# Routing traced in portions of 2.8 instead of 1.4, and gathered expert rows shared out anew between two halves of a PEER stage

## The chip, the cores and the metric

The kernel runs on one core of one Trainium2 chip. The metric is the device time of one execution in microseconds. All the times of the kernel before come from three timed runs and from one further execution that was profiled.

## The reference, cut to what matters

One decoder layer for 512 tokens of width 2048 in float32: a normalised input projection, two groups of attention heads, an output projection, and then a retrieval of experts (PEER) that is added to the result. Only the last matters here:

```python
def peer(h, w_q, sub_keys, expert_u, expert_v):
    q = (xt @ w_q).reshape(T, PEER_HEADS, 2, PEER_DQ // 2)
    s = jnp.einsum('thpd,hpnd->thpn', q, sub_keys)
    s_half, i_half = lax.top_k(s, PEER_TOPK)
    cand = s_half[:, :, 0, :, None] + s_half[:, :, 1, None, :]
    ...
    top_s, pos = lax.top_k(cand, PEER_TOPK)
    idx = jnp.take_along_axis(cand_idx, pos, axis=-1)
    g = jax.nn.softmax(top_s, axis=-1)
    ...
        u = expert_u[ic]
        a = jnp.einsum('cd,ced->ce', xc, u)
        w = (gc * jax.nn.gelu(a)).astype(xc.dtype)
        return jnp.einsum('ce,ced->cd', w, expert_v[ic])
```

Each token picks 8 x 16 = 128 of 16,384 experts. An expert has a row of `peer_u` and a row of `peer_v`, each of 2048 floats.

## The kernel before, in words

The four blocks of 128 tokens are treated in two ways. For block 0 (tokens 0 to 127) the chosen rows are fetched one slot at a time: an indirect DMA on the POOL queue (L965) brings 128 rows, one for each token, 1 MB in all, into one of three buffers `gt`. Slots 0 to 127 fetch rows of `peer_u`; VectorE forms a product with the tokens and its sum (L973, a multiply-and-reduce followed by a short read of the accumulator). Then comes one GELU (L978), and slots 128 to 255 fetch rows of `peer_v`, which VectorE adds to the result `h` (L976). These 256 steps are the generator `gathered()`. Step i asks first for the rows of step i + 2, whose buffer comes free when step i - 1 is done with it.

For blocks 1 to 3 (384 tokens, `TD`) every expert is computed densely, in two stages:

- The **U stage** is 128 blocks `u_block(e)`. One block loads 128 experts of `peer_u` (1 MB, on the SP and ACT queues, L858, two blocks ahead), VectorE transposes them in two halves (L870), ScalarE and VectorE split each half into a high and a low part (L117 and L118 in `split`), and TensorE multiplies them with the tokens: 16 steps of three matmuls with 384 columns (L883 to L885). A GELU (L890) follows, and its result goes to a scratch tensor in memory (L891, POOL queue). The halves are made three halves ahead of their matmuls (`u_turn(n + 3)`).
- The **V stage** is 16 groups of 8 such blocks. Each group multiplies `peer_v` (1024 rows, in four column pieces of 512) with weights `wg`, which are read back from the scratch tensor (L1015), multiplied by the gates on POOL (L1040), and split on ScalarE and VectorE. A group has 288 matmuls with 512 columns (L191 to L193), and VectorE adds each finished piece to the result (L1059, 12 in a group).

The gates for the dense part are made meanwhile by the generator `dense_gates()`: one-hot rows on POOL (L907), VectorE (L909) and ScalarE (L912), and two matmuls with 128 columns for each of 384 tokens (L922).

The generators are traced in pieces between other code. A `Filler` keeps a credit: `run(budget)` adds the budget, up to 4.0, and takes pieces from its queue until the credit is used up. A gathered step costs 2.3.

```python
            yield 2.3
    gatherer = Filler(paced=True)
    while filler.queue or later:
        flush(4)
        u_block(e, 1.4)
    share = 36.0 / (NK - 4 - e)
        u_block(e, share, 0.85)
                gatherer.run(1.6)
```

`u_block(e, budget, pace)` runs `filler` with `budget` and `gatherer` with `pace`, once in each of its two halves. The first loop runs until the routing (top-16 selections, `route`, L750 to L791) is traced; only then are `gathered()` and `dense_gates()` put into their queues. In the V stage the gatherer runs 16 times in a group. What is left after the last group is done by `gatherer.drain()`. A scheduler that knows the tiles decides the order of each engine's instructions from the order of the trace; a paced step is, besides, kept behind the last split or result addition (`mark`) that was traced before it.

Of the kernel before, what the change touches and what calls it, by code (L numbers as in the profile page):

```python
# [52 lines left out]
def block_kernel(ctx, tc, x, positions, norm1_gain, w_in, q_a_gain, w_q_b, kv_a_gain, w_kv_b, mla_q_gain,  # L53
# [13 lines left out]
    def pool(name, bufs=1, side=None, stack=ctx, **kw):  # L67
        return stack.enter_context(tc.tile_pool(name=name, bufs=bufs, side=side, reuse_waits="tile", **kw))
# [7 lines left out]
    def acc_tile(name="acc"):  # L76
        return psum.tile([128, 512], F32, name=name, tag="acc", bufs=5)

    def tp_tile(name="tp"):
        return psum.tile([128, 512], F32, name=name, tag="tp", bufs=3)  # L80
# [71 lines left out]
    def flush(n=None):  # L152
        for _ in range(len(later) if n is None else min(n, len(later))):
            later.pop(0)()
# [14 lines left out]
    def weights(src, kc, c0, n, by_row=False, turn=0):  # L169


        rows_of = src.rearrange("(i k j) n -> i j k n", i=4, j=32) if by_row else src.rearrange("(k p) n -> p k n", p=128)
        for k0 in range(0, kc, 4):
            kn = min(4, kc - k0)
            raw = raw_tile(turn * kc // 4 + k0 // 4)
            with tc.high_priority(offset=1500):
                if by_row:
                    for i in (0, 2, 1, 3):
                        nc.sync.dma_start(raw[32 * i:32 * i + 32, :kn, :n], rows_of[i, :, k0:k0 + kn, c0:c0 + n])
                else:  # L180
                    nc.sync.dma_start(raw[:, :kn, :n], rows_of[:, k0:k0 + kn, c0:c0 + n])
            for k in range(0, kn, 2):
                hi, lo = part_pair(turn * kc // 2 + (k0 + k) // 2, [128, 2, 512])
                with tc.high_priority(offset=1500):
                    split(hi[:, :, :n], lo[:, :, :n], raw[:, k:k + 2, :n])
                yield hi, lo

    def products(o, lhs, t, k0, kc, w, n):
        for k in range(2):
            kk = k0 + k  # L190
            nc.tensor.matmul(o, lhs(0, kk, t), w[0][:, k, :n], start=kk == 0, stop=False)  # L191
            nc.tensor.matmul(o, lhs(0, kk, t), w[1][:, k, :n], start=False, stop=False)  # L192
            nc.tensor.matmul(o, lhs(1, kk, t), w[0][:, k, :n], start=False, stop=kk == kc - 1)  # L193
# [668 lines left out]
    def u_turn(n):  # L862
        if n >= 2 * NK:
            return
        e, hf = divmod(n, 2)
        if hf == 0:
            u_load(e + 2)
        hi, lo = part_pair(n, [128, 8, 128])
        uT = up.tile([128, 8, 128], F32, name="uT")
        nc.vector.transpose(uT.rearrange("p k (b j) -> p b k j", j=32),  # L870
                            u_raw[e].rearrange("p b (k i) -> p b k i", k=KC)[:, :, hf * 8:hf * 8 + 8, :])
        split(hi, lo, uT)
        u_parts[n] = hi, lo

    def u_block(e, budget, pace=0.0):
        pa = acc_tile("pa")
        for hf in range(2):
            n = 2 * e + hf
            u_turn(n + 3)
            hi, lo = u_parts.pop(n)  # L880
            for k in range(8):
                kk = hf * 8 + k
                nc.tensor.matmul(pa[:, :TD], hi[:, k, :], xTd[0][:, kk, :], start=kk == 0, stop=False)  # L883
                nc.tensor.matmul(pa[:, :TD], hi[:, k, :], xTd[1][:, kk, :], start=False, stop=False)  # L884
                nc.tensor.matmul(pa[:, :TD], lo[:, k, :], xTd[0][:, kk, :], start=False, stop=kk == KC - 1)  # L885
            filler.run(budget)
            gatherer.run(pace)
        ga = xtp.tile([128, TD], F32, name="ga", bufs=2)
        with tc.issue_after(first[0].ins):
            nc.scalar.activation(ga, pa[:, :TD], AF.Gelu_apprx_tanh)  # L890
        nc.gpsimd.dma_start(acts_d[e], ga)  # L891
# [91 lines left out]
    gatherer = Filler(paced=True)  # L983
# [5 lines left out]
    e = 0  # L989
    while filler.queue or later:  # L990
        flush(4)
        u_block(e, 1.4)
        e += 1
    filler.add(settle())
    filler.add(first_tokens())
# [7 lines left out]
    share = 36.0 / (NK - 4 - e)  # L1003
    gts, wgs, wb = {}, {}, {}

    def gate_tile(g):
        if g < NSG:
            gg = wp.tile([128, TD, SG], F32, name="gg", bufs=2)
            nc.sync.dma_start(gg, gates_d[g].rearrange("j (t e) -> j t e", e=SG))
            gts[g] = gg  # L1010

    def act_tile(e):
        if e < NK:
            wgs[e] = wp.tile([128, TD], F32, name="wg", bufs=AHEAD)
            nc.sync.dma_start(wgs[e], acts_d[e])  # L1015
# [1 line left out]
    AHEAD = 5  # L1017
    wp = None
    while e < NK:
        u_block(e, share, 0.85)  # L1020
        e += 1
        if not filler.queue and wp is None:
            stg.close()
            wp = pool("wp", side="right")
            gate_tile(0)
            for i in range(AHEAD):
                act_tile(i)
# [5 lines left out]
    def w_block(e):  # L1033
        if e >= NK:
            return
        g, i = divmod(e, SG)
        if i == 0:
            gate_tile(g + 1)
        wg = wgs.pop(e)
        nc.gpsimd.tensor_tensor(wg, wg, gts[g][:, :, i], op=ALU.mult)  # L1040
        wb[e] = [dp.tile([128, TD], F32R, name=x, bufs=SG + 5) for x in ("wh", "wl")]
        split(wb[e][0], wb[e][1], wg)
        act_tile(e + AHEAD)
# [6 lines left out]
    for g in range(NSG):  # L1050
        for c in range(4):
            acc = [acc_tile(), acc_tile(), tp_tile()]
            for i, w in enumerate(weights(v_rows[g * SG * 128:(g + 1) * SG * 128], SG, c * 512, 512, turn=4 * g + c)):
                k0 = 2 * i
                for t in range(NT - 1):
                    products(acc[t], lambda hl, kk, t: wb[g * SG + kk][hl][:, t * 128:(t + 1) * 128], t, k0, SG, w, 512)
                    if k0 == SG - 2:
                        hc = h[t + 1][:, c * 512:(c + 1) * 512]
                        mark[0] = nc.vector.tensor_tensor(hc, acc[t], hc, op=ALU.add)  # L1059
                        if g == NSG - 1:  # L1060
                            nc.sync.dma_start(out[(t + 1) * 128:(t + 2) * 128, c * 512:(c + 1) * 512], hc)
                nxt = (g + 1) * SG
                if c < 3 and k0 < 4:
                    w_block(nxt + 2 * c + k0 // 2)
                if c == 3 and k0 > 2:
                    w_block(nxt + 4 + k0 // 2)
                gatherer.run(1.6)
    gatherer.drain()


# [23 lines left out]
```

## Time and profile before

| | |
|---|---|
| median of 3 runs | 3233.54 us (3232.82 to 3234.42) |
| the profiled execution's own time | 3233.09 us |
| its span in the profile | 3231.4 us |
| TensorE matmuls busy | 3104.4 us, 96% of the span |
| VectorE (DVE) busy | 2367.1 us, 73% |
| ScalarE (ACT) busy | 1271.4 us, 39% |
| GpSimd (POOL) busy | 1248.2 us, 39% |
| moved by DMA | 731.74 MB, 226 GB/s over the span |

The span counts from the first to the last instruction and transfer of the program. A matmul counts as busy until its modelled end, and matmuls overlap, so a busy TensorE can still have small gaps between two starts. How many matmuls a stretch holds tells more than its busy time. In the profile the U stage ends at about 2089 us, and the V stage follows.

### The profile page before, as it was taken

How to read it: one execution, taken by the hardware profiler on the slowest of the kernel's cores; microseconds unless marked ns; L12 is line 12 of the kernel's file. 1: busy time of each engine (PE TensorE's matmuls, PEld its weight loads, DVE VectorE, ACT ScalarE, POOL GpSimd, SP SyncE). 2: the span in 40 equal slices, each digit the busy share in tenths (PEclk: the TensorE clock that was granted, in tenths of full speed). 3: DMA queues.
4: the chain of work that ended last, by engine and by line, in shares of the span. 5: the costliest groups of instructions: out<-in, count | busy, mean ns of one | idle time of the engine just before them, and what ended most of it. 6: DMA issues, size and time to landing. Idle time of an engine off the chain costs nothing.

```text
span 3231.4 us, 43988 instructions
## 1 busy us (share of the span) xinstructions
PE 3104.4 (96%) x15802; PEld 2716.9 (84%) x15802; DVE 2367.1 (73%) x3502; ACT 1271.4 (39%) x2342; POOL 1248.2 (39%) x1260
## 2 busy tenths in 40 slices
PE   8999999989988999999999999999998999999997
PEld 6977768868788999999999999977776778887785
DVE  6436663247998567778778777788877989989896
ACT  5434452232234335566656554332222233222321
POOL 1115330001223015556566654254434445544542
PEclk9999999999999999999999999999999999999998
DMA  5422223243336668898879889998887999989896
GB/s 169 120 88 72 63 92 105 91 134 75 75 95 189 153 152 246 255 246 249 261 217 268 253 242 274 313 343 311 321 315 296 344 336 340 347 331 366 328 330 253
DMA packets 307068, 731.74 MB, mean 226 GB/s; under 512 B 24098, under 2 KB 106274, under 8 KB 269730
## 3 DMA queue, kind: packets, MB, share of 16 engines
q1 hardware_dynamic: 175394, 343.01, 33.8%
q0 software_dynamic: 45056, 293.63, 24.8%
q10 hardware_dynamic: 86400, 92.29, 10.9%
q8 instruction: 125, 2.05, 0.3%
q14 instruction: 93, 0.76, 0.1%
HBM read 666.97 MB, written 61.87 MB: 226 GB/s over the span
## 4 chain that ended last, share of the span: by engine, by line
PE 51%; DVE 13%; DMA 7%; issue 5%; POOL 2%; ACT 1%; ACTq 0%; SPq 0%; DVEq 0%; POOLq 0%
PE pa L883 10%; PE pa L885 10%; PE pa L884 10%; PE acc L192 4%; PE acc L193 4%; PE acc L191 4%; DMA wg<-acts_d 3%; DVE wlo L118 2%; PE gps L922 2%; DVE h L976 2%; PE tp L191 2%; PE tp L192 2%; PE tp L193 2%; DMA gt<-in_peer_u_dram,eidx 1%; DVE ulo L118 1%
## 5 line engine op out<-in xcount | busy, mean ns | idle before, releaser
L885 PE MATMUL pa<-xTd,wlo 128*128 128x384 f32 x1536 | 517.8, 339 | 12.5 <-DVE wlo L118 12.4
L883 PE MATMUL pa<-xTd,whi 128*128 128x384 f32 x1536 | 523.9, 341 | 0.2 <-ACT whi L117 0.2
L884 PE MATMUL pa<-xTd,whi 128*128 128x384 f32 x1536 | 519.1, 338 | 0.0
L118 DVE TENSOR_TENSOR wlo<-wraw,whi 128x1024 fp32r<-128x1024 f32 (+3 forms) x229 | 287.8, 1263 | 268.7 <-ACT whi L117 262.2
L907 POOL TENSOR_SCALAR oj<-iot,slT 128x128 fp32r<-128x128 f32 x384 | 351.4, 924 | 311.8 <-PE gps L922 310.4
L117 ACT ACTIVATE whi<-wraw 128x1024 fp32r<-128x1024 f32 (+3 forms) x229 | 232.6, 1022 | 503.6 <-PE acc L193 251.2
L973 DVE CUSTOM_DVE_ANT_0 gt<-gt,xn 128x2048 f32<-128x2048 f32 x128 | 297.6, 2325 | 53.9 <-DMA gt<-in_peer_u_dram,eidx 53.8
L976 DVE SCALAR_TENSOR_TENSOR h<-gt,w,h 128x2048 f32<-128x2048 f32 x128 | 319.7, 2497 | 18.3 <-DMA gt<-in_peer_v_dram,eidx 18.1
L118 DVE TENSOR_TENSOR wlo<-uT,whi 128x1024 fp32r<-128x1024 f32 x192 | 238.1, 1246 | 125.6 <-ACT whi L117 123.5
L192 PE MATMUL acc<-wlo,wh 128*128 128x512 f32 x768 | 306.7, 399 | 15.4 <-DVE wlo L118 15.3
L965 POOL DMA_INDIRECT gt<-in_peer_v_dram,eidx x128 | 220.2, 1720 | 256.7 <-DVE h L976 223.6
L1040 POOL TENSOR_TENSOR wg<-wg,gg 128x384 f32<-128x384 f32 x128 | 228.8, 1800 | 225.5 <-DMA wg<-acts_d 213.3
L191 PE MATMUL acc<-whi,wh 128*128 128x512 f32 x768 | 305.6, 398 | 5.0 <-ACT wh L117 5.0
L193 PE MATMUL acc<-whi,wl 128*128 128x512 f32 x768 | 305.4, 398 | 0.4 <-DVE wl L118 0.4
L885 PEld LDWEIGHTS pa<-xTd,wlo 128*128 128x128 f32 x1536 | 290.7, 189 | 13.9 <-DVE wlo L118 13.9
L883 PEld LDWEIGHTS pa<-xTd,whi 128*128 128x128 f32 x1536 | 291.3, 190 | 0.4 <-ACT whi L117 0.3
L884 PEld LDWEIGHTS pa<-xTd,whi 128*128 128x128 f32 x1536 | 291.0, 189 | 0.0
L912 ACT ACTIVATE oi<-on,gT 128x128 fp32r<-128x128 bf16 x768 | 250.6, 390 | 95.7 <-issue 24.4
L117 ACT ACTIVATE whi<-uT 128x1024 fp32r<-128x1024 f32 x192 | 200.8, 1053 | 141.0 <-PE pa L884 35.6
L965 POOL DMA_INDIRECT gt<-in_peer_u_dram,eidx x128 | 176.0, 1375 | 180.8 <-DVE a L973 158.8
L191 PE MATMUL acc<-whi,xT 128*128 128x512 f32 (+2 forms) x624 | 238.9, 383 | 4.7 <-ACT xT L117 2.3
L192 PE MATMUL acc<-wlo,xT 128*128 128x512 f32 (+2 forms) x624 | 233.5, 374 | 8.5 <-DVE wlo L118 8.4
(300 smaller groups left out, 6790.1 us busy)
## 6 DMA issues: line engine op xcount, KB each, us to landing
wraw<-in_peer_v_dram SPq DMA_DIRECT2D x86, 1024.0 KB
wraw<-in_peer_u_dram ACTq DMA_DIRECT2D x172, 256.0 KB
wraw<-in_peer_u_dram SPq DMA_DIRECT2D x172, 256.0 KB
uraw<-in_peer_v_dram SPq DMA_DIRECT2D x42, 1024.0 KB
acts_d<-ga POOLq DMA_DIRECT2D x128, 192.0 KB
gates_d<-stage ACTq DMA_DIRECT2D x24, 1024.0 KB
gg<-gates_d SPq DMA_DIRECT2D x16, 1536.0 KB
wg<-acts_d SPq DMA_DIRECT2D x128, 192.0 KB
```

Of the source, the lines that this page charges most:

```text
L117: first[0] = nc.scalar.activation(hi, src, AF.Copy)
L118: mark[0] = nc.vector.tensor_tensor(lo, src, hi.bitcast(F32), op=ALU.subtract)
L191: nc.tensor.matmul(o, lhs(0, kk, t), w[0][:, k, :n], start=kk == 0, stop=False)
L192: nc.tensor.matmul(o, lhs(0, kk, t), w[1][:, k, :n], start=False, stop=False)
L193: nc.tensor.matmul(o, lhs(1, kk, t), w[0][:, k, :n], start=False, stop=kk == kc - 1)
L883: nc.tensor.matmul(pa[:, :TD], hi[:, k, :], xTd[0][:, kk, :], start=kk == 0, stop=False)
L884: nc.tensor.matmul(pa[:, :TD], hi[:, k, :], xTd[1][:, kk, :], start=False, stop=False)
L885: nc.tensor.matmul(pa[:, :TD], lo[:, k, :], xTd[0][:, kk, :], start=False, stop=kk == KC - 1)
L907: nc.gpsimd.tensor_scalar(oj, iot, slT[1][:, t:t + 1], None, op0=ALU.is_equal)
L965: nc.gpsimd.indirect_dma_start(out=gt, out_offset=None, in_=u_rows if i < SLOTS else v_rows, in_offset=bass.IndirectOffsetOnAxis(ap=eidx0[ ...
L973: nc.vector.tensor_tensor_reduce(out=gt, in0=gt, in1=xn0, scale=1.0, scalar=0.0, op0=ALU.mult, op1=ALU.add, accum_out=a[:, s:s + 1])
L976: nc.vector.scalar_tensor_tensor(h[0], gt, w[:, s:s + 1], h[0], op0=ALU.mult, op1=ALU.add)
```

## The change

Three numbers change. The first loop of U blocks gives routing 2.8 for each half block instead of 1.4, so that it takes about half as many blocks. The second loop gives the gatherer 1.2 for each half block instead of 0.85. The V stage gives it 1.3 instead of 1.6 in each of its 16 turns in a group. `share`, the dense gates' part of each half block, is computed from the block that the second loop begins with, and so becomes smaller by itself.

```diff
@@ -989,7 +989,7 @@
     e = 0
     while filler.queue or later:
         flush(4)
-        u_block(e, 1.4)
+        u_block(e, 2.8)
         e += 1
     filler.add(settle())
     filler.add(first_tokens())
@@ -1017,7 +1017,7 @@
     AHEAD = 5
     wp = None
     while e < NK:
-        u_block(e, share, 0.85)
+        u_block(e, share, 1.2)
         e += 1
         if not filler.queue and wp is None:
             stg.close()
@@ -1064,7 +1064,7 @@
                     w_block(nxt + 2 * c + k0 // 2)
                 if c == 3 and k0 > 2:
                     w_block(nxt + 4 + k0 // 2)
-                gatherer.run(1.6)
+                gatherer.run(1.3)
     gatherer.drain()
```

The order of instructions shows it at three places of VectorE's queue. In it `uT` is a transposed half of a U block, `whi`/`wlo` and `uhi`/`ulo` are its parts, `on` a one-hot row of the dense gates, and `xn` the tokens of block 0. The first place is the U stage at blocks 22 to 24, before the change:

```order
 L870 STREAM_TRANSPOSE uT<-wraw 128x4x8x32 x2
 L118 TENSOR_TENSOR ulo<-uT,uhi 128x1024
 L118 TENSOR_TENSOR wlo<-uT,whi 128x1024
 L870 STREAM_TRANSPOSE uT<-wraw 128x4x8x32
 L870 STREAM_TRANSPOSE uT<-uraw 128x4x8x32
 L118 TENSOR_TENSOR wlo<-uT,whi 128x1024 x2
```

and with it:

```order
 L870 STREAM_TRANSPOSE uT<-wraw 128x4x8x32 x2
 L909 TENSOR_SCALAR on<-iotb,slT_9235 128x128 x4
 L118 TENSOR_TENSOR ulo<-uT,uhi 128x1024
 L118 TENSOR_TENSOR wlo<-uT,whi 128x1024
 L973 ISA gt,a<-gt,xn_5857 128x2048
 L973 ISA a 128x1
 L870 STREAM_TRANSPOSE uT<-wraw 128x4x8x32
 L870 STREAM_TRANSPOSE uT<-uraw 128x4x8x32
```

Gates and gathered rows now stand there from block 16 on instead of block 32. Counted up to the last transpose of the U stage, VectorE has 72 steps L973 before and 116 with the change. Up to the tenth block, where the routing ends, its queue reads the same in both. The second place is the third group of the V stage, before:

```order
 L973 ISA gt,a<-gt,xn_5857 128x2048
 L973 ISA a 128x1
 L118 TENSOR_TENSOR ulo<-uraw,uhi 128x1024
 L118 TENSOR_TENSOR wl<-wg,wh 128x384
 L973 ISA gt,a<-gt,xn_5857 128x2048
 L973 ISA a 128x1
 L118 TENSOR_TENSOR wlo<-wraw,whi 128x1024
 L118 TENSOR_TENSOR wl<-wg,wh 128x384 x2
 L973 ISA gt,a<-gt,xn_5857 128x2048
```

and with the change:

```order
 L118 TENSOR_TENSOR wl<-wg,wh 128x384 x3
 L118 TENSOR_TENSOR wlo<-wraw,whi 128x1024 x3
 L1059 TENSOR_TENSOR hd_21146<-acc,hd_21146 128x512
 L1059 TENSOR_TENSOR hd_21148<-acc,hd_21148 128x512
 L1059 TENSOR_TENSOR hd_21150<-tp,hd_21150 128x512
 L976 SCALAR_TENSOR_TENSOR h_4852<-gt,w,h_4852 128x2048
 L118 TENSOR_TENSOR ulo<-wraw,uhi 128x1024
 L976 SCALAR_TENSOR_TENSOR h_4852<-gt,w,h_4852 128x2048
```

Before, the rows of `peer_u` (L973) reach into the fifth group, 13 in the first and 9 to 12 in the others. With the change the last 12 of them stand in the first group, together with the GELU and the first row of `peer_v` (L976); then these rows follow at 9 in a group, where before there are mostly 11. The third place is the end of the program, before:

```order
 L1059 TENSOR_TENSOR hd_21014<-acc,hd_21014 128x512
 L1059 TENSOR_TENSOR hd_21016<-acc,hd_21016 128x512
 L1059 TENSOR_TENSOR hd_21018<-tp,hd_21018 128x512
 L976 SCALAR_TENSOR_TENSOR h_4852<-gt,w,h_4852 128x2048 x5
 L1090 UNCONDITIONAL_BRANCH
```

and with the change:

```order
 L118 TENSOR_TENSOR ulo<-wraw,uhi 128x1024
 L1059 TENSOR_TENSOR hd_21146<-acc,hd_21146 128x512
 L1059 TENSOR_TENSOR hd_21148<-acc,hd_21148 128x512
 L1059 TENSOR_TENSOR hd_21150<-tp,hd_21150 128x512
 L1090 UNCONDITIONAL_BRANCH
```

The five gathered steps that stood behind the last result addition are gone from there; the last gathered step now stands early in the last group.

## Rows read from the trace of the kernel before

**Rows 1.** Windows: stretch, busy time and instructions of each engine, clock, DMA share, GB/s.

```profile
1068.00:1200.00 132.00, 132.00 (x766) 132.00 (x765) 74.39 (x67) 42.70 (x56) 11.00 (x20) 1.00 0.64 149
1425.00:2022.00 597.00, 596.45 (x3629) 596.07 (x3628) 448.95 (x612) 351.27 (x800) 349.68 (x381) 1.00 0.86 251
2022.00:2089.00 67.00, 65.95 (x381) 65.63 (x379) 55.52 (x48) 21.50 (x27) 22.77 (x21) 1.00 0.96 307
2089.00:2173.00 84.00, 78.88 (x327) 62.09 (x328) 63.29 (x64) 26.30 (x37) 40.49 (x28) 0.98 0.90 340
2173.00:2479.00 306.00, 283.01 (x1172) 223.05 (x1171) 245.06 (x237) 84.60 (x101) 124.84 (x79) 0.98 0.83 310
2479.00:2881.00 402.00, 400.35 (x1714) 321.03 (x1713) 359.85 (x279) 121.49 (x143) 203.46 (x111) 1.00 0.91 338
2881.00:3211.00 330.00, 327.70 (x1400) 262.04 (x1398) 287.42 (x226) 91.31 (x103) 145.70 (x85) 1.00 0.89 331
```

**Rows 2.** Windows of the gates' matmuls L922 alone: PE and weight loads.

```profile
1425.00:2022.00 597.00, 77.18 (x552) 81.40 (x552) 1.00 0.86 251
```

**Rows 3.** Windows of L973 alone (two instructions a step): VectorE.

```profile
1425.00:2022.00 597.00, 107.93 (x94) 1.00 0.86 251
2022.00:2089.00 67.00, 18.34 (x16) 1.00 0.96 307
2173.00:2479.00 306.00, 101.88 (x86) 0.98 0.83 310
```

**Rows 4.** Windows of L976 alone: VectorE.

```profile
2479.00:2881.00 402.00, 165.09 (x65) 1.00 0.91 338
```

**Rows 5.** Groups by line on VectorE, 1425 to 2022 us: busy, mean ns, idle before.

```profile
L118 DVE TENSOR_TENSOR wlo<-uT,whi 128x1024 fp32r<-128x1024 f32 x95 | 116.9, 1230 | 67.6 <-ACT whi L117 65.9 <-ACT ga L890 1.6
L973 DVE CUSTOM_DVE_ANT_0 gt<-gt,xn 128x2048 f32<-128x2048 f32 x47 | 107.5, 2288 | 0.0
L973 DVE DVE_READ_ACCUMULATOR2_ANT a<- 128x1 f32 x47 | 3.8, 81 | 0.0
```

**Rows 6.** Waits, 2173 to 2479 us: total, times, longest, in us.

```profile
DVE gt L973 <- DMA gt<-in_peer_u_dram,eidx: 46.4, 12, 7.5
...
PE acc L192 <- DVE wlo L118: 12.7, 7, 4.8
PE acc L192 <- DVE ulo L118: 10.2, 6, 4.9
```

**Rows 7.** Waits, 2479 to 2881 us.

```profile
DVE h L976 <- DMA gt<-in_peer_v_dram,eidx: 6.4, 5, 2.6
...
PE acc L192 <- DVE ulo L118: 1.6, 2, 1.2
```

**Rows 8.** Timeline, third V group: start, duration, engine, instruction, idle before.

```profile
2260.00 2.29 DVE L973 CUSTOM_DVE_ANT_0 gt<-gt,xn 128x2048 f32<-128x2048 f32 x1 [4.89 <-DMA gt<-in_peer_u_dram,eidx]
...
2258.30 0.40 PE L191 MATMUL acc<-whi,wh 128*128 128x512 f32 x1
2263.49 0.62 PE L192 MATMUL acc<-wlo,wh 128*128 128x512 f32 x1 [4.80 <-DVE wlo L118]
2263.91 0.63 PE L193 MATMUL acc<-whi,wl 128*128 128x512 f32 x1
```

**Rows 9.** Timeline, end of the program: VectorE, then the SP queue.

```profile
3210.61 0.69 DVE L1059 TENSOR_TENSOR hd<-tp,hd 128x512 f32<-128x512 f32 x1 [0.71 <-PE tp L193]
3211.22 7.12 DVE L976 SCALAR_TENSOR_TENSOR h<-gt,w,h 128x2048 f32<-128x2048 f32 x3
...
3224.09 2.35 DVE L976 SCALAR_TENSOR_TENSOR h<-gt,w,h 128x2048 f32<-128x2048 f32 x1 [0.26 <-DMA gt<-in_peer_v_dram,eidx]
...
3194.53 17.13 SPq L1061 DMA_DIRECT2D out_dram<-hd  x4
3226.47 0.33 SPq L981 DMA_DIRECT2D out_dram<-h  x1
```

**Rows 10.** One line's instructions, L973: shortest, median and longest ns.

```profile
L973 DVE CUSTOM_DVE_ANT_0 gt<-gt,xn x128: 2272/2284/3957, 1007.9 to 2459.5; 128x2048 f32<-128x2048 f32 x128
```

## The prediction

> **What bounds the kernel now.** I read the windows first, because the change moves work between two stages. In the U stage TensorE is the bound. The stretch from 1068 to 1200 us has neither gates nor more than one gathered row: 766 matmuls in 132 us, 0.1723 us each [rows 1]. From 1425 to 2022 us gates and rows are added. Of its 3629 matmuls 552 are the gates' [rows 1, 2]. The other 3077 at 0.1723 us make 530.2 us, and the remaining 66.8 us are less than the 77.2 us for which the gate matmuls count as busy. So there is no room for stalls. VectorE is busy for 449 of these 597 us, 75% [rows 1]; its 47 gathered steps found their data there each time (no idle time before them), while it waited 65.9 us for ScalarE's high parts [rows 5]. A wait there costs nothing as long as the parts are ready ahead of TensorE.
>
> In the V stage the same count shows where time is lost. From 2479 us to 3211 us there are 1714 + 1400 = 3114 matmuls in 732 us, 0.2351 us each. From 2173 to 2479 us there are 1172, which would be 275.5 us at that pace, and it took 306: **30.5 us lost**. The first group, 2089 to 2173 us, has 327 matmuls, 76.9 us at that pace: 7.1 us lost [rows 1]. The waits name the cause in the slow stretch. VectorE waited 46.4 us in 12 waits for gathered rows of `peer_u`, and TensorE waited for VectorE's low parts, 12.7 and 10.2 us [rows 6]. One case can be followed in the timeline: a step L973 sat 4.89 us until its rows landed, the split behind it in the queue came late, and TensorE stood from 2258.3 to 2263.5 us. After it matmuls start 0.42 us apart [rows 8], nearly twice the usual spacing, which is the lower of the clock's two levels (1.2 instead of 2.4 GHz); the granted clock of the stretch is 0.98. In the next stretch, 2479 to 2881 us, rows are even denser, 65 steps in 402 us [rows 4] against 43 in 306 [rows 3], yet VectorE waited 6.4 us for them and TensorE 1.6 us for VectorE [rows 7].
>
> At the end the last result addition is over at 3211.3 us. Five gathered steps follow, the last begins at 3224.09 us, the write of `h` is issued at 3226.47 us, and the span ends at 3231.4 us [rows 9]. That is a **tail of 20.1 us** after the last work of the dense part.
>
> **The change, part by part.** No instruction is added or removed; the 256 gathered steps, the routing and the gates stay as many as they were.
>
> *Routing in larger portions.* VectorE's queue is the same up to the end of the routing, so nothing is gained there directly. Its effect is that gates and rows start some 16 blocks earlier, in a stretch where VectorE is busy 56% and the DMA engines 64% of the time [rows 1]. The gates' matmuls cost TensorE the same wherever they stand: 0.
>
> *44 more steps in the U stage.* The order has 116 instead of 72 up to the last transpose. One costs VectorE 2.288 + 0.081 = 2.37 us [rows 5], together 104 us. They are spread over about 112 blocks, some 1020 us. Before there were 47 steps in 597 us, now 116 in 1020; that is 0.035 more per us and 8% more of VectorE, so 83%. There is a stretch that shows this load already: from 2022 to 2089 us there are 8 steps in 67 us [rows 3], VectorE is busy 55.5 us, 83%, and 381 matmuls at 0.1723 us fill 65.6 of the 67 us [rows 1]. The bounds are 0 and 104 us (each added step paid in full). That nearest row loses 1.4 us in 67, part of which is the change of stage; scaled to 1020 us it gives 21 us as a cautious value. I take **+4 us**, near the lower end, because 1425 to 2022 us shows no loss at all.
>
> *Their transfers.* A step brings 1.05 MB, so 0.035 more per us adds 37 GB/s to 251. The 288 GB/s are below the 307 that the stretch from 2022 to 2089 us carries without a stall, and below the 338 of the V stage [rows 1]. 0. On POOL each added gather stands between the gates' one-hot rows; POOL is busy 350 of 597 us [rows 1], and in the idle 41% of 1020 us each of 44 added steps could take 9 us. 0. If that cover fails, it shows as gate matmuls that come late, and TensorE has other matmuls between them.
>
> *Groups 2 to 5 of the V stage.* All rows of `peer_u` but 12 are gone from the stage; at 9 rows of `peer_v` in a group it has fewer than the later groups have now. I price these groups at the pace of the later ones, and leave a little for waits like those of [rows 7] (6.4 us in 402, so some 4 in 306): 30.5 - 4 = **26.5 us gained**. The bounds are 0 and 30.5.
>
> *The first group.* It keeps 12 of 13 steps L973, and takes in the GELU, which waits for the last of them and stands on ScalarE ahead of later splits. Gates that end some blocks earlier may help. Between a gain of the 7.1 us lost there now and one more wait as long as the longest, 7.5 us [rows 6]; I take 0.
>
> *The later groups.* 9 steps instead of 11 give VectorE more air, but TensorE sets the pace there already: 0.
>
> *The tail.* The last addition is followed by the write of a quarter of a megabyte instead of five steps and the write of 1 MB. That write took 4.9 us; I take 4 us for the smaller one, between 0 and 4.9. 20.1 - 4 = **16 us gained**.
>
> The sum is 4 - 26.5 + 0 - 16 = -38.5 us on the profiled execution's 3233.1 us, **3195 us** rounded. That execution lies 0.45 us under the median of the runs. The forecast's own range is 3180 (no loss in U, the first group smooth, nothing lost in groups 2 to 5: 4 + 7.1 + 4 us less) to 3212 us (21 us lost in U instead of 4).
>
> **The rivals.** *First: the slow groups are slow because they begin the V stage, not because of the rows of `peer_u`.* For it speaks that denser rows do no harm later [rows 4, 7], so something else must differ, as the first weights `wg` that have to come back from memory. Against it: the waits name `peer_u` transfers, and it is a long start that lasts four groups. Then only the tail is gained: 3233.1 - 16 + 4 = 3221 us.
>
> *Second, and slower: in the U stage VectorE is already the pace-maker behind the scenes.* Its idle quarter is then no room but a loop with ScalarE (a transpose, the high part, the low part), with 65.9 us of waits in 597 [rows 5], and an added step lengthens the block. Paid in full that is 104 us against the 42.5 gained: 3233.1 - 42.5 + 104 = 3295 us. It decides once more than 42.5 of 104, 41%, are exposed. Against it speak the matmul counts above, above all 2022 to 2089 us.
>
> *Third: VectorE and POOL hinder each other.* A step L973 takes 2284 ns in the median and 3957 at most [rows 10], so something can stretch it by 1.67 us. If all 116 in the U stage were stretched like that, VectorE would have 194 us more in 1020, 19% on top of 83%, and the stage would be 2% over, some 26 us: 3233.1 - 42.5 + 26 = 3217 us. Against it: the mean in the U stage is 2288 ns [rows 5] with POOL busy more than half the time. The Trainium skill, "SBUF — State Buffer", section "SBUF: two separate sides", states a rule of this kind: an instruction of VectorE with two SBUF inputs and a GpSimd instruction that reads SBUF take an exclusive lock on one shared port pair, and the loser waits for the whole instruction. By that rule more such steps beside the one-hot rows of POOL would be longer; the mean of this trace does not bear it out for these.
>
> **How the numbers follow.** Forecast 0.70, first rival 0.13, second 0.09, third 0.03. The remaining 0.05 is for gains and losses that cancel to within 0.2% (6.5 us), about what a measurement of this kernel can tell from no change. So faster 0.70 + 0.13 + 0.03 = 0.86, the same 0.05, slower 0.09. The range reaches from 3176 to 3225 us: it takes in the forecast's own range, the third rival and the first, and leaves out the slower one and the cancelling cases.
>
> **What would show it.** Right: L973 between the U blocks from about block 16, with a mean under 2.4 us; the U stage's matmuls without gates still at 0.172 to 0.174 us; the last addition L1059 as the last work of VectorE, followed by one write; from the second V group on about 0.235 us for each matmul, and no long waits for gathered rows. Wrong: TensorE waiting for low parts in the U stage (second rival); groups 2 to 5 still losing 30 us without L973 in them (first rival); L973 well over 2.4 us there (third).

## The result, and the profile of the changed kernel

The changed kernel takes 3204.56 us in the median of four runs (3198.46 to 3209.73), the kernel before 3233.18 us on the same chip (3230.99 to 3234.42). The ratio is 0.9912 with a 95% interval of 0.989 to 0.9933: **0.9% faster**. The forecast was 3195 us, so it is 9.6 us too low. The profiled execution took 3209.73 us with a span of 3207.7 us, 23.7 us less than before. It is the slowest of the four; where the others were faster, up to 11.3 us, no profile shows.

The windows of the changed kernel, with the same columns as [rows 1]; the stages are cut where its U stage (2114 us) and its V groups end:

```profile
1200.00:2035.00 835.00, 818.49 (x4891) 814.80 (x4890) 669.41 (x850) 442.41 (x977) 436.90 (x497) 0.99 0.92 279
2035.00:2114.00 79.00, 78.88 (x456) 78.56 (x454) 66.94 (x59) 24.28 (x30) 22.09 (x20) 1.00 0.97 287
2114.00:2208.00 94.00, 83.62 (x341) 64.48 (x342) 74.30 (x71) 29.64 (x42) 48.59 (x30) 0.98 0.88 334
2208.00:2469.00 261.00, 261.00 (x1120) 210.07 (x1119) 227.32 (x179) 81.04 (x95) 116.06 (x69) 1.00 0.87 323
2469.00:2869.00 400.00, 400.00 (x1716) 321.93 (x1715) 329.74 (x267) 122.93 (x142) 159.39 (x98) 1.00 0.83 307
2869.00:3204.00 335.00, 334.81 (x1435) 269.11 (x1433) 248.94 (x209) 93.56 (x105) 109.70 (x65) 1.00 0.73 268
```

Counted in matmuls, as the prediction counted, this is where the 23.7 us come from:

| stretch | before | changed | difference |
|---|---|---|---|
| end of the U stage | 2089 us | 2114 us | +25 |
| first V group, beyond its matmuls | 84 us - 327 x 0.2351 = 7.1 lost | 94 us - 341 x 0.2332 = 14.5 lost | +7.4 |
| groups 2 to 5, beyond their matmuls | 30.5 lost | 0 (1120 x 0.2332 = 261.2 in 261 us) | -30.5 |
| pace of the V stage, some 4612 matmuls | 0.2351 us each | 996 us / 4271 = 0.2332 | -8.6 |
| after the last addition L1059 | 20.1 us | 3.2 us | -16.9 |

The last three are gains as forecast, or more. From the second group on TensorE waits for nothing, and of the gathered rows VectorE waits only this (waits of the changed kernel, 2208 to 3204 us):

```profile
DVE h L976 <- DMA gt<-in_peer_v_dram,eidx: 16.5, 8, 3.2
```

At the end no gathered step is left (the changed kernel's timeline, VectorE and the SP queue; compare [rows 9]):

```profile
3203.84 0.69 DVE L1059 TENSOR_TENSOR hd<-tp,hd 128x512 f32<-128x512 f32 x1 [0.71 <-PE tp L193]
...
3201.76 3.14 SPq L1061 DMA_DIRECT2D out_dram<-hd  x3
```

The U stage lost 25 us where the forecast had 4. The added steps are not stretched, and wait for nothing: from 1200 to 2035 us VectorE's groups have L973 at 2298 ns, with no idle time before it (compare [rows 5]).

```profile
L973 DVE CUSTOM_DVE_ANT_0 gt<-gt,xn 128x2048 f32<-128x2048 f32 x93 | 213.7, 2298 | 0.0
L118 DVE TENSOR_TENSOR wlo<-uT,whi 128x1024 fp32r<-128x1024 f32 x134 | 164.2, 1239 | 95.2 <-ACT whi L117 95.2
```

It is ScalarE that is late. Its waits in the same stretch, and TensorE's for it, are (the releaser "issue" means that ScalarE waited for nothing that the profile shows):

```profile
ACT whi L117 <- issue: 74.2, 14, 11.8
...
ACT uhi L117 <- issue: 56.5, 10, 11.6
...
PE pa L883 <- ACT whi L117: 11.8, 7, 4.9
...
PE pa L883 <- ACT uhi L117: 4.7, 1, 4.7
```

One case in the timeline of the changed kernel, first ScalarE with its queue, then TensorE:

```profile
1307.20 0.39 ACTq L932 DMA_DIRECT2D gates_d<-stage  x1
1308.37 11.01 ACTq L858 DMA_DIRECT2D wraw<-in_peer_u_dram  x2
1319.43 2.00 ACT L117 ACTIVATE whi<-uT 128x1024 fp32r<-128x1024 f32 x2 [12.26 <-DMA gates_d<-stage]
...
1314.75 1.00 PE L922 MATMUL gps<-oi,oj 128*128 128x128 f32 x8
1320.54 0.69 PE L883 MATMUL pa<-xTd,whi 128*128 128x384 f32 x1 [4.79 <-ACT whi L117]
```

L932 writes a tile of gates to memory, 1 MB in pieces of 512 bytes, on ScalarE's queue. Directly behind it stand two loads of the next U blocks, L858. Issuing them normally takes ScalarE 0.44 us each; here the pair took 11.01 us. ScalarE makes no high part in that time, and TensorE, whose parts are asked for three halves ahead, has none left some 7 us after the hold began. (The row of ScalarE's high part names the write as what ended its 12.26 us of idle time; the two issues account for 11.01 of them.) The stall has a second price. Windows right after it:

```profile
1320.50:1322.50 2.00, 1.96 (x5) 1.49 (x6) 1.98 (x2) 2.00 (x5) 0.39 (x1) 0.50 0.50 138
1322.50:1324.50 2.00, 2.00 (x7) 2.00 (x7) 2.00 (x2) 2.00 (x7) 0.25 (x1) 0.50 0.29 108
1324.50:1327.00 2.50, 2.50 (x11) 2.50 (x11) 2.50 (x4) 0.13 (x1) 1.00 (x1) 0.61 0.00 0
```

After it the granted clock is 0.50, the lower of the two levels, for 4 us, and 0.61 in the 2.5 us that follow. The 23 matmuls from 1320.5 to 1327 us would take 4.0 us at 0.1723 and took 6.5. So such a stall costs 4.8 + 2.5, some 7 us. There are three of this size (from 1315.8, 1516.3 and 1752.5 us), 22 us together: the three sets of eight blocks that hold them take 80 to 82 us, the others there 73 to 74.

### The profile page after: what moved, and what is told of

The parts are those of the page before. It is cut to its first block, busy times and chain, and to the rows that moved or that the text cites. A ratio compares the mean times of both kernels' runs of the same rounds, so it can differ in the third digit from the quotient of the medians.

```text
span 3207.7 us, 43873 instructions
## 1 busy us (share of the span) xinstructions
PE 3104.4 (97%) x15802; PEld 2721.3 (85%) x15802; DVE 2363.0 (74%) x3502; ACT 1267.4 (40%) x2342; POOL 1189.6 (37%) x1260
## 4 chain that ended last, share of the span: by engine, by line
PE 59%; DVE 10%; issue 3%; DMA 3%; ACTq 2%; ACT 1%; POOL 1%; DVEq 0%; SPq 0%; POOLq 0%
PE pa L883 8%; PE pa L885 8%; PE pa L884 8%; PE acc L191 8%; PE acc L193 7%; PE acc L192 7%; PE tp L191 4%; PE tp L193 3%; PE tp L192 3%; PE gps L922 2%; ACTq L858 2%; DVE wlo L118 2%; DVE uT L870 2%; DMA wraw<-in_peer_u_dram 1%; DVE gt L973 1%
## 5 line engine op out<-in xcount | busy, mean ns | idle before, releaser
L907 POOL TENSOR_SCALAR oj<-iot,slT 128x128 fp32r<-128x128 f32 x384 | 338.9, 891 | 355.3 <-PE gps L922 355.2
L976 DVE SCALAR_TENSOR_TENSOR h<-gt,w,h 128x2048 f32<-128x2048 f32 x128 | 320.2, 2502 | 16.5 <-DMA gt<-in_peer_v_dram,eidx 16.5
L965 POOL DMA_INDIRECT gt<-in_peer_v_dram,eidx x128 | 201.8, 1577 | 351.7 <-DVE h L976 319.4
L973 DVE CUSTOM_DVE_ANT_0 gt<-gt,xn 128x2048 f32<-128x2048 f32 x128 | 299.0, 2336 | 3.6 <-DMA gt<-in_peer_u_dram,eidx 3.6
L912 ACT ACTIVATE oi<-on,gT 128x128 fp32r<-128x128 bf16 x768 | 240.7, 390 | 66.5 <-PE gps L922 66.2
L191 PE MATMUL acc<-whi,xT 128*128 128x512 f32 (+2 forms) x624 | 238.4, 382 | 4.3 <-ACT xT L117 2.3
L193 PE MATMUL acc<-whi,xT 128*128 128x512 f32 (+2 forms) x624 | 236.1, 378 | 0.0
```

Of the source, the lines that this page charges most:

```text
L907: nc.gpsimd.tensor_scalar(oj, iot, slT[1][:, t:t + 1], None, op0=ALU.is_equal)
L912: nc.scalar.activation(oi[:, r, :], on, AF.Copy, scale=gT[r][:, t:t + 1].bitcast(F32))
L973: nc.vector.tensor_tensor_reduce(out=gt, in0=gt, in1=xn0, scale=1.0, scalar=0.0, op0=ALU.mult, op1=ALU.add, accum_out=a[:, s:s + 1])
L976: nc.vector.scalar_tensor_tensor(h[0], gt, w[:, s:s + 1], h[0], op0=ALU.mult, op1=ALU.add)
```

## The experiments

Three theories for the loss in the U stage. The **queue theory**: ScalarE is held at the loads behind the gates' write. The **VectorE theory**: the added steps alone eat the lead, as the second rival had it. The **theory of the transfers**: the DMA engines, busy 92% of the stretch, are full, and all U loads come late.

### Where the gates' write is issued

`e1_gates_sp` is the changed kernel with that write on the SP queue, where nothing computes.

```diff
             if tb == GT - 4:
-                nc.scalar.dma_start(
+                nc.sync.dma_start(
```

> The changed kernel with one edit: the 24 writes of finished gates (1 MB each, in pieces of 512 bytes) are issued from the SP queue instead of ScalarE's. Queue theory (in the U stage ScalarE is held while it issues the U loads that stand right behind such a write in its own queue, up to 11 us, and TensorE runs out of parts): the three stalls of some 5 us of the U stage go, its end comes back from 2115 to 2090-2097 us, no issue of a U load on ScalarE's queue takes over 2 us, the time is 3180-3190 us, and the runs lie closer together than the 11 us of the changed kernel. VectorE theory (44 more steps L973 are too much for VectorE): nothing changes, 3198-3210 us. DMA theory (the transfers of the U stage are at the limit of the DMA engines, whoever issues them): the stalls move to waits for U loads, 3198-3210 us.

Measured: 3190.84 us (3188.43 to 3199.15), ratio 0.9859 (0.9828 to 0.9891). Its windows:

```profile
1200.00:2035.00 835.00, 831.87 (x5013) 830.97 (x5012) 700.33 (x866) 451.70 (x983) 368.86 (x503) 1.00 1.00 288
```

Both kernels have 640 gate matmuls L922 in this stretch; these are two answers of the windows for L922 alone, first of the changed kernel, then of this one:

```profile
1200.00:2035.00 835.00, 80.31 (x640) 82.84 (x640) 0.99 0.92 279
```

```profile
1200.00:2035.00 835.00, 80.29 (x640) 82.83 (x640) 1.00 1.00 288
```

So the changed kernel is short of 5013 - 4891 = 122 dense matmuls, 21.0 us at 0.1723. That agrees with the 22 us of three stalls. The durations of the issues (shortest, median and longest ns) show the hold move from ScalarE to SP. First before, then changed, then this kernel:

```profile
L858 ACTq DMA_DIRECT2D wraw<-in_peer_u_dram x172: 317/444/5293, 851.6 to 2051.3; - x172
```

```profile
L858 ACTq DMA_DIRECT2D wraw<-in_peer_u_dram x172: 317/444/9244, 852.9 to 2079.5; - x172
```

```profile
L858 ACTq DMA_DIRECT2D wraw<-in_peer_u_dram x172: 317/378/1846, 853.2 to 2054.2; - x172
L858 SPq DMA_DIRECT2D wraw<-in_peer_u_dram x172: 311/432/9142, 869.7 to 2054.2; - x172
```

The U stage ends at 2092 us, 3 us later than before; with the 22 us of the stalls that makes the 25 us. VectorE is busier than in the changed kernel (700 us of 835) and the DMA engines are busy all the time, yet the stalls are gone. Neither of these can be the whole cause.

`a0_changed_again` and `a1_gates_sp_again` are the changed kernel and `e1_gates_sp` once more, on one chip.

> The changed kernel as it is, once more, beside the next two on one chip. Queue theory: 3198-3210 us, with runs that differ by some 10 us, as the holding of ScalarE's queue does or does not exceed the lead. If the 14 us that separate it from the first run were a difference of chips, it would come out at 3188-3195 us here.

> The first run's kernel (the changed kernel with the gates' writes on the SP queue) once more: 3187-3196 us, 10-16 us under the changed kernel of this call. If both come out alike, the queue theory has shown the stalls but not the time.

Measured: 3206.93 us (3200.12 to 3214.48; ratio 0.9916, 0.9892 to 0.9939) and 3193.58 us (3190.57 to 3204.07; ratio 0.988, 0.9856 to 0.9904). The difference is 13.4 us again. Their windows:

```profile
1200.00:2035.00 835.00, 820.31 (x4917) 817.10 (x4916) 670.49 (x852) 441.75 (x977) 455.10 (x498) 0.99 0.93 280
```

```profile
1200.00:2035.00 835.00, 829.00 (x4989) 826.80 (x4988) 694.71 (x861) 446.93 (x975) 373.28 (x502) 1.00 1.00 285
```

Here 72 matmuls are missing, 12.4 us. The spread of the runs, 14.4 us with the holds on ScalarE and 13.5 without, did not shrink, against what was expected of `e1_gates_sp`; nothing here shows that these holds set runs of one kernel apart.

`e6_before_gates_sp` makes the same edit in the kernel before.

> The kernel before with one edit: the gates' writes on the SP queue. Queue theory: before, the issues behind a write hold ScalarE 5.3 us at most, which the parts made ahead cover, so little is to be gained: 3226-3236 us. If the writes cost the kernel before something too, which its matmul count does not show, up to 20 us faster.

Measured: 3233.48 us, ratio 0.9991 (0.9977 to 1.0006). The holds of up to 5.3 us there were covered by the lead, and moving them gains nothing. The place of the write matters only with the change.

`e2_uload_sp` is the changed kernel with the loads taken away from behind the write instead: all four pieces of a U load on SP.

```diff
-                for i, queue in ((0, nc.sync), (2, nc.scalar), (1, nc.sync), (3, nc.scalar)):
+                for i, queue in ((0, nc.sync), (2, nc.sync), (1, nc.sync), (3, nc.sync)):
```

> The changed kernel with one other edit: all four pieces of a U load are issued from the SP queue, none from ScalarE's; the gates' writes stay on ScalarE's queue. Queue theory: nothing stands behind a gates' write on ScalarE's queue any more, so the stalls go as in the first run, 3180-3190 us; if a full queue rather than ScalarE's standing were what hurts, SP is held instead and loads come late. VectorE theory and DMA theory: 3198-3210 us.

Measured: 3518.5 us, ratio 1.0869 (1.0836 to 1.0902), a miss by far. Waits from 1200 to 2300 us, VectorE's group of transposes from 1200 to 2280 us, and a window after the last gate matmul:

```profile
ACT oi L912 <- PE gps L922: 441.2, 83, 9.7
...
PE pa L883 <- ACT whi L117: 151.2, 65, 2.8
```

```profile
L870 DVE STREAM_TRANSPOSE uT<-wraw 128x1024 f32<-128x1024 f32 x116 | 137.0, 1217 | 0.0
```

```profile
2278.00:2345.00 67.00, 67.00 (x381) 67.00 (x380) 62.74 (x56) 20.98 (x26) 20.19 (x18) 0.98 1.01 301
```

While the gates are made, eight blocks take 96 to 102 us instead of 73 to 82. The loads are not what is late: VectorE has next to no idle time before its transposes, and once the gates are done, blocks 112 to 119 take 69 us with all their loads still on SP, and TensorE waits for nothing. What grew is ScalarE's waiting for the gate matmuls (62.8 us in the changed kernel, 1200 to 2035 us) and with it TensorE's waiting for ScalarE. With the edit the scheduler put ScalarE's queue in another order: the GELU of a finished block now stands between two high parts that stood together before. That this order makes the ring of waits is inferred. The run tells nothing between the theories, since it changes more than the queue of the loads.

### Why the holds became long, and why they show

`e5_short_l973` keeps every transfer of the changed kernel and shortens VectorE's added work; `e10_narrow_u_rows` keeps most of that work and shortens the transfers.

```diff
-                nc.vector.tensor_tensor_reduce(out=gt, in0=gt, in1=xn0, scale=1.0, scalar=0.0, op0=ALU.mult,
+                nc.vector.tensor_tensor_reduce(out=gt[:, :256], in0=gt[:, :256], in1=xn0[:, :256], scale=1.0, scalar=0.0, op0=ALU.mult,
```

> The changed kernel with VectorE's part of a peer_u step cut to 256 of 2048 columns (so seven eighths of each of block 0's products are left out); the transfers stay whole. The gates' writes stay on ScalarE's queue. Theory that the added transfers lengthen the holding of ScalarE's queue: stalls of some 5 us stay in the U stage, its end at 2105-2115 us, and the time stays at 3196-3208 us (a few us better in the first V group, where 12 of these steps stand). Theory that VectorE's added work leaves too little lead to bridge the holding (which would be the same length before and after): the U stage ends near 2090 us, 3175-3187 us.

```diff
-                nc.gpsimd.indirect_dma_start(out=gt, out_offset=None, in_=u_rows if i < SLOTS else v_rows,
+                nc.gpsimd.indirect_dma_start(out=gt[:, :n], out_offset=None, in_=u_rows.rearrange("a (b c) -> (a b) c", c=512) if i < SLOTS else v_rows,
...
-                nc.vector.tensor_tensor_reduce(out=gt, in0=gt, in1=xn0, scale=1.0, scalar=0.0, op0=ALU.mult,
+                nc.vector.tensor_tensor_reduce(out=gt[:, 512:].rearrange("p (a n) -> p a n", a=3), in0=gt[:, None, :512].to_broadcast([128, 3, 512]), in1=xn0[:, 512:].rearrange("p (a n) -> p a n", a=3), scale=1.0, scalar=0.0, op0=ALU.mult,
```

> The changed kernel with the transfers of the peer_u steps cut to a quarter (512 columns of a row of a view with shorter rows, so block 0's products are of other rows and leave a quarter of the columns out), VectorE's part to three quarters (1536 columns, some 1.7 us). The gates' writes stay on ScalarE's queue. Transfer theory: the issues behind a gates' write hold ScalarE no longer than about 3 us, no stall of 5 us in the U stage, its end near 2090 us, 3175-3190 us. VectorE theory: only a quarter of the effect goes, the U stage ends at 2105-2112 us, 3195-3205 us.

Measured: 3180.77 us (ratio 0.9834, 0.9806 to 0.9861) and 3183.14 us (0.9837, 0.9813 to 0.9861). The first still has an issue of 10.3 us, but 16 over 2 us on ScalarE instead of 24. Its stage is nearly smooth; the one stall left, 4.0 us at 2008.7 us, is not at a write:

```profile
L858 ACTq DMA_DIRECT2D uraw<-in_peer_u_dram x84: 317/408/10302, 867.5 to 2041.0; - x84
```

```profile
1200.00:2035.00 835.00, 831.04 (x4997) 830.14 (x4996) 516.90 (x858) 448.24 (x978) 415.81 (x504) 1.00 0.97 285
```

In the second the issues stay short:

```profile
L858 ACTq DMA_DIRECT2D wraw<-in_peer_u_dram x172: 317/444/3546, 854.4 to 2050.9; - x172
```

```profile
1200.00:2035.00 835.00, 834.67 (x5039) 834.04 (x5038) 645.48 (x870) 452.00 (x986) 395.98 (x506) 1.00 0.77 199
```

So the long holds come with the gathers' transfers: with these at a quarter no issue takes over 3.5 us. Their place counts too. In both traces of the changed kernel four pairs of issues behind a write take 7.1 to 11.4 us, and just there a gather L965 was issued 2.9 to 5.3 us before the write. At the other twenty the last gather lies 6.2 to 7.6 us back, and the pair takes at most 5.7 us. This was not tested by a run of its own, and it is not a full rule: in `a1_gates_sp_again` a pair on SP took 12.4 us with the gather 7.0 us back.

Why long holds become stalls shows in the lead, counted in the traces: the high parts finished, less the halves (24 matmuls, 4.6 us with their share of gates) that TensorE has begun, when a write between 1200 and 2035 us is issued. In the mean it is 2.5 halves before, 1.7 in the changed kernel, in `e1_gates_sp` and in `e10_narrow_u_rows`, and 3.0 in `e5_short_l973`. 1.7 halves are some 7.8 us: more than the usual pair of issues, less than the three of 11 us. That VectorE's added work is what shortens the lead is argued and not shown: in `e5_short_l973` the scheduler also put ScalarE's queue in another order, and in `e10_narrow_u_rows`, with a quarter less of that work, the lead is the same. Long holds and the short lead together are harmless in `e1_gates_sp`, where the hold sits on another engine. The times of these two runs are not to be had, since they come from less work; they show causes.

### The two parts of the change

`e3_only_portions` is the kernel before with one line of the change, `e4_only_paces` with the other two.

```diff
-        u_block(e, 1.4)
+        u_block(e, 2.8)
```

> The kernel before with only the larger routing portions (2.8), the paces stay 0.85 and 1.6. By the order, 83 steps L973 stand before the last transpose (72 before, 116 with the whole change), rows of peer_u reach into the fourth V group, and no gathered step stands behind the last addition. All theories: the tail of 20 us shrinks to 4 (-16). Theory that the peer_u rows make the early V groups slow: groups 2 to 4 still lose some 20 of 30 us (-8). Queue theory: U loss of 0-10 us, because the DMA engines are less loaded. Sum 3205-3217 us. Start-up theory (the early V groups are slow whatever rows stand there) is refuted by the changed kernel already; it would give 3217 here.

Measured: 3223.3 us (3216.49 to 3235.51, 10 runs), ratio 0.9963 (0.9944 to 0.9981): under half of the gain, and 6 us above the expected range. Windows over its first V group and over groups 2 to 5:

```profile
2094.00:2186.00 92.00, 80.37 (x326) 62.59 (x327) 69.72 (x67) 25.60 (x37) 42.14 (x28) 0.96 0.84 316
2186.00:2470.00 284.00, 271.16 (x1135) 215.06 (x1134) 238.32 (x219) 82.42 (x97) 121.85 (x74) 0.98 0.86 322
```

At 0.2351 us for each matmul the first group loses 15.4 us, where before it lost 7.1, and groups 2 to 5 lose 17.2 of the 30.5 us. So groups 2 to 5 came out as expected, and the first group is what the expectation left out. Earlier portions without a faster pace leave rows of `peer_u` in groups 2 to 4, at 11, 13 and 8, and these groups take 79, 75 and 70 us.

```diff
-        u_block(e, share, 0.85)
+        u_block(e, share, 1.2)
...
-                gatherer.run(1.6)
+                gatherer.run(1.3)
```

> The kernel before with only the two paces changed (1.2 and 1.3), routing portions stay 1.4. By the order, 102 steps L973 stand before the last transpose, the peer_u rows end in the third V group, but 8 gathered steps stand behind the last addition instead of 5. Tail: about 3 us for each of three more steps, +8 us. Early V groups: 22 of 30 us gained. U stage: the same density of rows and gates as in the changed kernel over 96 instead of 112 blocks; queue theory: up to 20 us lost; no loss would mean that the position of the gates' writes in the queue matters and not the load. Sum 3219-3240 us.

Measured: 3233.81 us, ratio 0.9998 (0.998 to 1.0016). It has the long holds, and some of the lost matmuls; and with fewer rows later and no earlier start, eight gathered steps are left at the end. Its issues, and the last addition and the last write in its timeline:

```profile
L858 ACTq DMA_DIRECT2D uraw<-in_peer_u_dram x84: 317/444/11065, 869.2 to 2059.0; - x84
```

```profile
3200.01 0.69 DVE L1059 TENSOR_TENSOR hd<-tp,hd 128x512 f32<-128x512 f32 x1 [0.71 <-PE tp L193]
...
3224.46 0.33 SPq L981 DMA_DIRECT2D out_dram<-h  x1
```

From 3200.7 us to the end of its span at 3229.7 us are 29 us, where before there are 20.1. Its U stage ends 20 us late, at 2109 us. Those 20 us and the 9 us more at the end take back the 30.6 us that the stretch between them gains (3200.7 - 2109 = 1091.7 us, before 3211.3 - 2089 = 1122.3). The two parts need each other: the portions make room in time, the paces fill it.

### Two versions that were to beat `e1_gates_sp`

`e7_gates_sp_denser` is `e1_gates_sp` with other paces, so that no row of `peer_u` is left in the V stage.

```diff
-        u_block(e, share, 1.2)
+        u_block(e, share, 1.4)
...
-                gatherer.run(1.3)
+                gatherer.run(1.15)
```

> The changed kernel with the gates' writes on the SP queue, and paces 1.4 and 1.15 instead of 1.2 and 1.3: by the order all 128 steps of peer_u and 12 of peer_v stand in the U stage, 8 in each V group, none behind the last addition. Against the first run (3191 us): the first V group loses its 12 steps L973 and the wait for the GELU, some 5-7 us; the U stage keeps its 73.6 us for 8 blocks if neither VectorE (about 86% busy) nor the DMA engines (some 300 GB/s) become the bound. Then 3183-3187 us. If the U stage has reached its limit with 8.5 rows in 8 blocks, it loses: each added step paid in full would be 24 steps x 2.4 = 57 us, 3240 us.

Measured: 3205.47 us, ratio 0.9909 (0.9884 to 0.9933): worse than the two sets of `e1_gates_sp` by 15 and 12 us. Its U blocks hold their pace with 9 or 10 rows for eight blocks until about 1960 us. Then one stall comes: ScalarE stands at its own two U loads, issued at 1966.7 and 1971.8 us, and the trace names the first read of the gates as what ended the wait (waits, 1960 to 2040 us):

```profile
ACT uhi L117 <- DMA gg<-gates_d: 17.5, 1, 17.5
...
PE pa L883 <- ACT uhi L117: 7.1, 1, 7.1
```

Its first V group still takes 95 us, without any L973 in it. The profiled execution, 3196.22 us, is the fastest of the four, 7.8 us above that of `e1_gates_sp`, and its U stage ends 7.6 us later; why the other three took 8 to 12 us more, no profile shows.

`e8_ahead8` is `e1_gates_sp` with the weights `wg` asked for eight blocks ahead instead of five.

```diff
-    AHEAD = 5
+    AHEAD = 8
...
-        wb[e] = [dp.tile([128, TD], F32R, name=x, bufs=SG + 5) for x in ("wh", "wl")]
+        wb[e] = [dp.tile([128, TD], F32R, name=x, bufs=SG + 4) for x in ("wh", "wl")]
```

> The first run's kernel with 8 instead of 5 tiles wg loaded ahead (and one buffer fewer for the split weights, so that it fits). Theory that the first V group loses some 14 us mainly because the last of its 8 weights wg come back from memory only after the U stage: 5-8 us under the kernel of the second run, 3182-3186 us. If the first group's loss comes from its 12 steps L973 and the GELU, nothing changes within 2 us. By the order the second tile of gates now stands ahead of U loads on the SP queue, which could hold those back: then the U stage ends some us later.

Measured: 3194.86 us, ratio 0.9879 (0.9856 to 0.9902), no gain. The first V group fell to 87 us with 318 matmuls, 12 us lost at 0.2332 instead of 17 in `a1_gates_sp_again`, but the U stage ended at 2102 us instead of 2094: the second tile of gates is now read on SP ahead of U loads, and blocks 112 to 119 took 79 us instead of 75. The best version stays `e1_gates_sp`, with ratios of 0.9859 and 0.988 in two sets of runs.

## Why the prediction was right, and where it was off

- **Tail, -16**: -16.9. The write at the end took 3.2 us where 4 was taken.
- **Groups 2 to 5, -26.5**: -30.5. The few waits for rows that were allowed for never reach TensorE, and nothing is lost there.
- **Later groups, 0**: mis-sized, about -6 of the -8.6 us. The pace 0.2351 was taken for TensorE's own. With 9 gathered steps in a group instead of 11 it is 0.2332, and TensorE's last short waits are gone. `e4_only_paces` has the same: 3090 matmuls from 2479 to 3200 us against 3068 before. `e3_only_portions`, which keeps the pace of 1.6 there, has 2492 from 2550 to 3140 us, the changed kernel 2531.
- **First V group, 0**: +7.4, at the upper bound of 7.5. Counted in matmuls at 0.2332, `e5_short_l973` loses 4.8 us there and `e10_narrow_u_rows` 12.3, so VectorE's work for its twelve L973 seems to count more than their transfers. But the group also loses some 15 us in `e7_gates_sp_denser` without any L973, and 16 in `e4_only_paces` with as many as before. In the changed kernel ScalarE waits there for POOL's weights, and these for their transfer (waits, 2114 to 2208 us):

```profile
ACT wh L117 <- POOL wg L1040: 30.2, 9, 10.2
...
POOL wg L1040 <- DMA wg<-acts_d: 20.9, 3, 10.2
```

  Before, these two waits are nearly as long (29.1 and 19.4 us, 2089 to 2173 us), so they do not explain the 7.4 us. The cause stays open.
- **U stage, +4**: +25, **the step that failed**. The sum priced 44 steps on VectorE and 37 GB/s on the DMA engines, each against its own idle time. With the hold taken off ScalarE (`e1_gates_sp`) the same steps and transfers cost 3 us, so these two prices were about right. What the sum left out is a third resource: the time ScalarE spends issuing loads behind the gates' write, which both of them change. The trace of before showed it, in the issues of 5.3 us and in rows like this of its waits from 1068 to 2089 us, which the prediction did not read:

```profile
ACT whi L117 <- issue: 33.9, 12, 4.9
```

  [Rows 5] even name the victim: VectorE's 65.9 us of waiting for high parts. The prediction took them for slack; that part of them was lead being used up is an inference from these runs.

Of the rivals, the **first** (the early groups are slow because they begin the stage) falls: with no L973 groups 2 to 5 lose nothing, and `e3_only_portions` moves the loss along with the rows. For the first group alone it stays open. It is not the kind of row alone: in `e4_only_paces` the second group has 10 of them and runs 299 matmuls in 69.8 us, 0.2334 each; so their density counts too. The **second** (VectorE is the pace-maker in U) named the right stage and the right loop, but VectorE was not its bound; 25 of 104 us were paid, 22 of them in the three stalls at ScalarE's holds. The **third** falls: L973 beside POOL takes 2298 ns against 2288 before. The Trainium skill, "SBUF — State Buffer", section "SBUF: two separate sides", lets an instruction of VectorE with two SBUF inputs and a GpSimd instruction that reads SBUF lock each other out of a shared port. The trace agrees, but it is POOL that waits, which the prediction did not look at: a one-hot row L907 usually takes 0.60 us and up to 3.82, and the 39 that begin while an L973 runs take 2.25 us in the median (the changed kernel, 1200 to 2035 us; shortest, median and longest ns). TensorE had no wait for POOL in that stretch.

```profile
L907 POOL TENSOR_SCALAR oj<-iot,slT x311: 590/601/3818, 1204.6 to 1954.9; 128x128 fp32r<-128x128 f32 x156
```

The forecast of faster was right because the gains lie in the V stage, far from the missed term; they came out 13.5 us larger than priced (4, 8.6 and 0.9), the losses 28.4 us larger (21 and 7.4). The difference, 14.9 us, is the profiled execution's distance from 3195 us (14.7). That the number came this near is in part luck: two errors of opposite sign, 13.5 and 28.4 us, cancel by half.

## What to carry to other kernels

When a change makes transfers denser, look at the time each engine spends issuing DMAs as well as at the queues' bandwidth: rows in which a computing engine waits for "issue", and issues whose longest is ten times their median. A hold that the lead still covers costs nothing until other work shortens the lead, so price it together with that work. Here the write was better on a queue whose engine computes nothing, 13 us in both comparisons; there single loads behind it were held for up to 10.4 us as well, without such stalls of TensorE. The size of the write's pieces was not varied.

## What the runs showed of the hardware

A DMA issue of 0.44 us can hold its engine for up to 11 us when it stands behind a write of 1 MB in 512-byte pieces on the same queue (`e4_only_paces`, 11.1 us). The longest on one row of issues grew from 5.3 us before to 9.2 with the change, as the DMA engines went from 87% to 92% busy, and with the gathers' transfers at a quarter and the DMA engines at 77% it is 3.5.

One queue carries these loads at TensorE's pace: in `e2_uload_sp`, from 2278 to 2345 us, 40 pieces of 256 KB were issued on SP alone, its queue moved 8.8 MB, 131 GB/s, and TensorE waited for nothing. The Trainium skill, "DMA: Bandwidth & Descriptors", section "Rules for kernel authors", says that spreading DMAs over SP, ACT and GpSimd does not help bandwidth and only saves issue time. That stretch agrees with it; what this case adds is that the time of issuing can be what counts, 13 us of 3204.56 for one write's queue.

A step L973 of VectorE, with two inputs in SBUF, lengthens POOL's one-hot rows beside it from 0.60 to 2.25 us in the median, and is itself 2298 ns long in the mean against 2288 before.
